# Reading the 512 moving columns of a matmul in 64-byte pieces, and shifting the operand tiles by 256 bytes against one pool of weights

## The chip, the cores and the metric

The kernel runs on one core of one Trainium2 chip. The metric is the device time of one execution in microseconds, the median of several runs. A core has a matrix engine (PE, whose weight loads the profile lists apart as PEld), a vector engine (DVE), a scalar engine (ACT), a general engine (POOL) and a sync engine (SP) that issues transfers. SBUF is the on-chip memory of 128 partitions from which the engines read operands, and PSUM is the accumulator memory into which PE writes.

## The reference, cut to what matters

One decoder layer on 1024 positions of width 1024, in float32:

```
h = rmsnorm(x)
[q | k | v | u | s | gate_a | gate_b] = h @ w_in
A = sliding-window attention(q, k, v);  B = u * (tril(W_s) @ rmsnorm(s) + b)
x = x + (sigmoid(gate_a) * (A @ w_oa) + sigmoid(gate_b) * (B @ w_ob)) @ w_out
x = x + down( silu(conv_g) * conv_v ),  conv = causal depthwise width-3 conv of up(rmsnorm(x))
```

The MLP is 2816 wide, so `w_up` has 5632 columns and `w_down` 2816 rows. All matrix products together are what PE does; every other operation is elementwise, a row reduction or a softmax over 128 keys.

## The kernel before, in words

**Arithmetic on PE.** Every float32 operand of a large product is split into a high part (`copy_hi`, line 77, on ACT) and a low part (a subtraction on POOL or DVE), both of type fp32r. A product is then three matmuls with one output: high weights by high moving, high weights by low moving, low weights by high moving. [...] The profile's group name `pz<-T,qh` reads: output `pz`, moving tile `T`, weight tile `qh`.

**Three places issue the 512-column matmuls.** `mm3` (lines 79 to 83) issues the three for the `u` projection (`pu`), the two branch outputs (`po`) and the `w_out` product (`px`). `Blocks.prod` (lines 924 to 929) issues twelve, four depth steps of three, for one of the seven block products into which the gate projections and the up projection are cut; its outputs are `pz`. `mms` (lines 1620 to 1633) does the same for the down projection, outputs `pd` and `pdy`. `mm3` also issues matmuls of 256 columns (`pkv`, `pq`, `pvs`, `pm`), and line 505 those of the attention output (`pv`).

**Stages.** The order is: key, value and first query projections; attention mixed with the rest of the query and `u` projections; the second token mixer; the gates in eight pairs; the branch outputs and `w_out`; the up projection in 22 pairs, each with convolution and gating of the pair before on ACT, DVE and POOL; the down projection in seven steps of eleven depth tiles. The order of PE's instructions is written out by hand; what is prepared for it (loads on SP's queue, high parts on ACT, low parts on POOL and DVE) runs some tiles ahead.

**Where the operands lie.** SBUF is handed out in pools from the left in the order `base` (line 44), `big` (line 47), `wst` (line 48), then the pools of the stages (`ex` and `wx` among them); `edge`, `gp` and `zr` come from the right. Each pool follows the end of the one before. `base` ends in a filler tile, `base_pad` (line 125), which makes it 7680 bytes, or 15 times 512, long; `edge_pad` does the like on the right. The tiles of `big`, `wst`, `ex`, `wx`, `gp` and `zr` that PE reads have sizes that are multiples of 512 bytes, so in the kernel before every weight tile and every moving tile of a 512-column matmul begins at a multiple of 512 bytes. `big` holds the moving tiles of nearly all products (`x`, `T`, `B`, `mh`, `ml`, `bh`, `bl`, `ah` and `al` as moving tiles of `po`), the weights of the down projection (`ah`, `al`), and `AX`, the weights of two of the seven block products. `wst` holds the weights `wuh`, `wul`, `wjh`, `wjl`, `ph`, `pl`, `qh`, `ql`. `gp` holds the gates' weights `gax` and `s3h`, `s3l`; `wx` holds the up projection's `s3h`, `s3l`, whose moving tile `T3` lies in `ex`. In the gates that moving tile lies in `zr`. The attention's tiles `ch`, `cl`, `eh`, `el`, moving in `pv`, begin 192 bytes past a multiple of 512, and their weights `vhl` at a multiple of 512.

Of the kernel before, what the change touches and what calls it, by code (L numbers as in the profile page):

```python
# [10 lines left out]
F = mybir.dt.float32  # L11
# [23 lines left out]
def build(tc, a):  # L35
    nc = tc.nc
    ctx = ExitStack()
    with ctx, tc.manual_schedule(engines={mybir.EngineType.PE}):
        body(ctx, tc, nc, a)


def body(ctx, tc, nc, a):
    L, H = slice(0, 512), slice(512, 1024)
    base = ctx.enter_context(tc.tile_pool(name="base", bufs=1))
# [3 lines left out]
    wst = ctx.enter_context(tc.tile_pool(name="wst", bufs=2))  # L48
    uid = [0]
    psum = {}  # L50

    def nm(s):
        uid[0] += 1
        return f"{s}_{uid[0]}"
# [18 lines left out]
    def raw(s):  # L73
        return wst.tile([128, 8, 128], F, tag="raw", name=nm(s), bufs=3)

    def copy_hi(dst, src, scale=1.0):
        return nc.scalar.activation(dst, src, AF.Copy, scale=scale)  # L77

    def mm3(out, wh, wl, mh, ml, first, last, **kw):

        nc.tensor.matmul(out, wh, mh, start=first, stop=False, **kw)  # L81
        nc.tensor.matmul(out, wh, ml, start=False, stop=False, **kw)  # L82
        nc.tensor.matmul(out, wl, mh, start=False, stop=last, **kw)  # L83
# [9 lines left out]
    def wsplit(r, s, nk=8):  # L93

        h = wst.tile([128, 8, 128], R, tag="wh", name=nm(s + "h"))
        l = wst.tile([128, 8, 128], R, tag="wl", name=nm(s + "l"))
        copy_hi(h[:, :nk, :], r[:, :nk, :])
        nc.gpsimd.tensor_tensor(l[:, :nk, :], r[:, :nk, :], h[:, :nk, :].bitcast(F), op=ALU.subtract)  # L98
        return h, l
# [22 lines left out]
    nsink = base.tile([128, 8], F, name="nsink")  # L122
    ss_b = base.tile([128, 8], F, name="ss_b")
    vss8 = base.tile([128, 8], F, name="vss8")
    base.tile([128, 72], F, name="base_pad")

    def rms_rows(pb, diag, hs=(0, 1)):

# [43 lines left out]
    def rsplit(w, r, c):  # L172

        rv = r.rearrange("p (k a) b -> p k (a b)", a=2)
        ks = slice(4 * c, 4 * c + 4)
        copy_hi(w[:, 0, ks, :], rv)
        nc.gpsimd.tensor_tensor(w[:, 1, ks, :], rv, w[:, 0, ks, :].bitcast(F), op=ALU.subtract)
# [33 lines left out]
    for k in range(8):  # L211
        x1 = xr[k]
        copy_hi(wkv[:, 0, k, :], x1[:, 1:257])
        nc.vector.tensor_tensor(wkv[:, 1, k, :], x1[:, 1:257], wkv[:, 0, k, :].bitcast(F), op=ALU.subtract)
        for c in xcuts[k] if k in xcuts else (slice(0, 512), slice(512, 1024)):
            xc = x1[:, 257 + c.start:257 + c.stop]
            copy_hi(hx(0, k, c), xc, scale=x1[:, 0:1])
            nc.vector.scalar_tensor_tensor(hx(1, k, c), xc, x1[:, 0:1], hx(0, k, c).bitcast(F),
                                           op0=ALU.mult, op1=ALU.subtract)
        for s in range(8):  # L220
            o = pkv[s // 4][:, (s % 4) * 256:(s % 4 + 1) * 256]
            c = slice(s * 128, (s + 1) * 128)
            mm3(o, hx(0, k, c), hx(1, k, c), wkv[:, 0, k, :], wkv[:, 1, k, :],
                k == 0 and s % 2 == 0, k == 7 and s % 2 == 1)
        if k > 0:
            xsquare(k - 1)
        if k + X_AHEAD < 8:
            xload(k + X_AHEAD)
        if k == 2:
            rwq = rload(a["wq"][0], "wq")  # L230
            nc.sync.dma_start(ident, a["ident"])
            nc.sync.dma_start(cp, a["cp"])
        if k == 4:
            u_raw = [wload(a["wu"][0], "wu")]
            nc.sync.dma_start(sink_b, a["sink"])
            nc.sync.dma_start(ali, a["ali"])
        if k == 5:
            rsplit(wq[0], rwq[0], 0)
        if k == 6:
            rsplit(wq[0], rwq[1], 1)  # L240
# [7 lines left out]
    def q_proj(n):  # L248
        half, b = divmod(n, 8)
        w = wq[half]  # L250
        p = PH("pq")[:, 0:256]
        c = slice(b * 128, (b + 1) * 128)
        for k in range(8):
            mm3(p, hx(0, k, c), hx(1, k, c), w[:, 0, k, :], w[:, 1, k, :], k == 0, k == 7)
        st[("pq", n)] = p
# [49 lines left out]
    for s in range(8):  # L305
        nc.tensor.matmul(p_ssq[:, 2 * s:2 * s + 2], sqsum[:, s * 128:(s + 1) * 128], ones[:, 0:2],
                         start=True, stop=True)
# [216 lines left out]
    def u_chunk(i):  # L524
        t, j = divmod(i, 4)
        if j == 0:
            ust["p"] = PS("pu")
        p, (wh, wl) = ust["p"], ust[("w", t)]
        for k in (2 * j, 2 * j + 1):
            for h in range(2):  # L530
                c = slice(h * 512, (h + 1) * 512)
                mm3(p[:, c], wh[:, k, :], wl[:, k, :], hx(0, k, c), hx(1, k, c), k == 0, k == 7)
        return t if j == 3 else None
# [382 lines left out]
    class Blocks:  # L916
# [7 lines left out]
        def prod(self, o, l, r, more=False):  # L924
            (wh, wl), y = self.w[l], self.y[r]
            for k in range(4):
                for j, (p, q) in enumerate(((wh, 0), (wh, 1), (wl, 0))):
                    nc.tensor.matmul(o, p[:, k, :], y[:, q, k, :], start=not more and k == 0 and j == 0,  # L928
                                     stop=k == 3 and j == 2, skip_group_check=True)

        def temps(self):
# [598 lines left out]
    def mlp():  # L1530
# [81 lines left out]
        def banks():  # L1612
            psum["C"].__exit__(None, None, None)
            ps = ctx.enter_context(tc.tile_pool(name="psD", bufs=1, space=bass.MemoryType.PSUM, reuse_waits="tile"))
            X.extend(ps.tile([128, 512], F, tag=f"pd{i}", name=f"pd{i}") for i in range(4))
            for _ in range(2):
                p = psA.tile([128, 1024], F, tag="P", name=nm("pdy"))
                Yb.extend([p[:, L], p[:, H]])

        def mms(g):  # L1620
            s, k0, k1 = groups[g]
            ah, al, bh, bl = ops_.pop(g)
            if g == 0:
                banks()
            o = Yb if s in ("M2", "M7", "M4") else X
            new = s in ("M1", "M7")
            for k in range(k0, k1):
                for d in range(4):
                    m = slice(128 * d, 128 * d + 128)
                    for j, (p, q) in enumerate(((ah, bh), (ah, bl), (al, bh))):  # L1630
                        nc.tensor.matmul(o[d], p[:, k - k0, m], q[:, k - k0, :],  # L1631
                                         start=new and k == 0 and j == 0, stop=k == HK - 1 and j == 2,
                                         skip_group_check=True)

# [61 lines left out]
        prev, q, rms = first_pair()  # L1696
        for n in range(1, NPAIR):
            q = fast_pair(n, prev, q or Pair(n, lefts[n].w), (start0, start1, start), rms)
            prev, q, rms = q, None, None
        q = prev  # L1700
        n_load = 4
        for g in range(len(groups)):
            mms(g)
            s, k0, k1 = groups[g]
            while n_load < min(g + 6, len(groups)):
                loads(n_load)
                n_load += 1
            if g in SUM_AT:
                sum_loads(*GR[SUM_AT.index(g)])
            if k1 == HK:  # L1710
                done(s)
            if g == 0:
                q.tap_v()
                q.last_sum()
                q.conv_v()
                prep(2)
                q.tap_g()
                q.conv_g()
            if g == 1:
                q.gated()  # L1720
                q.stores()
                pools["ft_cm"].__exit__(None, None, None)
                pools["yd"] = ctx.enter_context(tc.tile_pool(name="yd", bufs=1, reuse_waits="tile"))
            if g + 3 < len(groups):
                prep(g + 3)
            if g - 2 in SUM_AT:
                sums2(*GR[SUM_AT.index(g - 2)])
            if g == 0:
                q.tanh()
# [73 lines left out]
```

## Time and profile before

| | |
|---|---|
| time, median of 3 runs | 1197.96 us (1197.24 to 1198.21) |
| the profiled execution | 1196.57 us |
| its span in the trace | 1194.4 us |
| PE busy | 1181.5 us, 5850 matmuls |
| PEld busy | 999.1 us, 5850 weight loads |
| DVE, ACT, POOL busy | 864.3, 550.3, 561.3 us |
| HBM traffic | 159 GB/s over the span |

The span is the time from the first to the last instruction in the trace; the execution's own time is 2.17 us longer. Busy time of an engine is the union of its instructions' times, so matmuls that overlap in the pipeline are not counted twice. The duration of one matmul is from its start to its modelled end, and the next one starts long before that: what a matmul costs is the distance between two starts.

### The profile page before, as it was taken

How to read it: one execution, taken by the hardware profiler on the slowest of the kernel's cores; microseconds unless marked ns; L12 is line 12 of the kernel's file. 1: busy time of each engine (PE TensorE's matmuls, PEld its weight loads, DVE VectorE, ACT ScalarE, POOL GpSimd, SP SyncE). 2: the span in 40 equal slices, each digit the busy share in tenths (PEclk: the TensorE clock that was granted, in tenths of full speed). 3: DMA queues.
4: the chain of work that ended last, by engine and by line, in shares of the span. 5: the costliest groups of instructions: out<-in, count | busy, mean ns of one | idle time of the engine just before them, and what ended most of it. 6: DMA issues, size and time to landing. Idle time of an engine off the chain costs nothing.

```text
span 1194.4 us, 15778 instructions
## 1 busy us (share of the span) xinstructions
PE 1181.5 (99%) x5850; PEld 999.1 (84%) x5850; DVE 864.3 (72%) x1010; ACT 550.3 (46%) x848; POOL 561.3 (47%) x359
## 2 busy tenths in 40 slices
PE   9999999999999999999999999999999999999998
PEld 8889989888888888888888888888888888888887
DVE  8688967754548665347897788878887798865674
ACT  8455565744345222445544444444444445434331
POOL 2467683577768322334756575756656551000000
PEclk9999999999999999999999999999999999999999
DMA  7010133137786997343142333423233358965471
GB/s 286 21 54 19 54 129 128 36 99 245 247 313 215 352 317 269 146 150 115 54 141 99 113 128 110 141 91 131 106 133 112 100 203 285 384 229 194 145 234 71
DMA packets 78988, 191.00 MB, mean 160 GB/s; under 512 B 8896, under 2 KB 9152, under 8 KB 78912
## 3 DMA queue, kind: packets, MB, share of 16 engines
q1 hardware_dynamic: 78912, 190.00, 45.9%
q8 instruction: 46, 0.75, 0.3%
q14 instruction: 30, 0.25, 0.1%
HBM read 139.38 MB, written 50.59 MB: 159 GB/s over the span
## 4 chain that ended last, share of the span: by engine, by line
PE 91%; DVE 3%; ACT 1%; issue 0%; POOL 0%; ACTq 0%; DVEq 0%
PE pz L928 48%; PE pd L1631 10%; PE pdy L1631 8%; PE px L83 2%; PE px L81 2%; PE po L81 2%; PE po L83 2%; PE po L82 2%; PE px L82 2%; PE pvs L81 1%; PE pvs L83 1%; PE pvs L82 1%; PE pv L505 1%; PE pq L81 1%; PE pq L83 1%; PE pq L82 1%
## 5 line engine op out<-in xcount | busy, mean ns | idle before, releaser
L928 PE MATMUL pz<-T,qh 128*128 128x512 f32 x480 | 148.1, 390 | 0.0
L887 POOL TENSOR_TENSOR pl<-lp,ph 128x1024 fp32r<-128x1024 f32 x30 | 72.5, 2417 | 92.9 <-ACT ph L77 92.8
L928 PE MATMUL pz<-B,ph 128*128 128x512 f32 x352 | 109.7, 393 | 0.0
L928 PEld LDWEIGHTS pz<-T,qh 128*128 128x128 f32 x480 | 89.9, 188 | 18.5
L928 PE MATMUL pz<-T,ql 128*128 128x512 f32 x240 | 93.4, 389 | 0.0
L98 POOL TENSOR_TENSOR wjl<-wj,wjh 128x512 fp32r<-128x512 f32 (+1 forms) x24 | 40.7, 1697 | 102.1 <-ACT wjh L77 99.2
L887 POOL TENSOR_TENSOR ql<-lq,qh 128x1024 fp32r<-128x1024 f32 x29 | 74.9, 2583 | 8.8 <-ACT qh L77 8.8
L928 PEld LDWEIGHTS pz<-B,ph 128*128 128x128 f32 x352 | 65.3, 188 | 15.9 <-ACT x L1479 2.4
L943 DVE TENSOR_TENSOR pz<-pz,rstd_b 128x1024 f32<-128x1024 f32 x60 | 73.9, 1232 | 2.1
L887 POOL TENSOR_TENSOR s3l<-s,s3h 128x512 fp32r<-128x512 f32 x30 | 41.2, 1373 | 71.5 <-ACT s3h L77 71.5
L928 PE MATMUL pz<-T,s3h 128*128 128x512 f32 x240 | 73.9, 389 | 0.0
L928 PE MATMUL pz<-B,pl 128*128 128x512 f32 x176 | 68.5, 389 | 0.0
L1631 PE MATMUL pd<-bh,ah 128*128 128x512 f32 x176 | 68.5, 389 | 0.0
L1631 PE MATMUL pd<-bl,ah 128*128 128x512 f32 x176 | 68.5, 389 | 0.0
L1631 PE MATMUL pd<-bh,al 128*128 128x512 f32 x176 | 68.5, 389 | 0.0
L928 PE MATMUL pz<-B,AX 128*128 128x512 f32 x264 | 63.4, 389 | 0.0
L928 PE MATMUL pz<-T,AX 128*128 128x512 f32 x264 | 63.4, 389 | 0.0
L928 PEld LDWEIGHTS pz<-B,AX 128*128 128x128 f32 x264 | 49.6, 188 | 10.3
L928 PEld LDWEIGHTS pz<-T,AX 128*128 128x128 f32 x264 | 49.6, 188 | 10.3
L1337 DVE SCALAR_TENSOR_TENSOR tg<-pz,cp,tg 128x1023 f32<-128x1023 f32 (+1 forms) x44 | 56.2, 1278 | 0.8
L1337 DVE SCALAR_TENSOR_TENSOR tv<-pz,cp,tv 128x1023 f32<-128x1023 f32 (+1 forms) x44 | 56.2, 1278 | 0.8
L77 ACT ACTIVATE qh<-lq 128x1024 fp32r<-128x1024 f32 (+1 forms) x31 | 32.0, 1036 | 52.2 <-issue 24.7
(329 smaller groups left out, 3502.5 us busy)
## 6 DMA issues: line engine op xcount, KB each, us to landing
ls<-wup SPq DMA_DIRECT2D x22, 512.0 KB, 5.5
sum<-ls SPq DMA_DIRECT2D x22, 512.0 KB, 5.1
lp<-wup SPq DMA_DIRECT2D x22, 512.0 KB, 3.5
ra<-wdown SPq DMA_DIRECT2D x44, 256.0 KB, 4.5
b<-T SPq DMA_DIRECT2D x44, 256.0 KB, 3.7
B<-tv SPq DMA_DIRECT2D x33, 256.0 KB, 2.0
T<-tt SPq DMA_DIRECT2D x33, 256.0 KB, 2.0
b<-B SPq DMA_DIRECT2D x33, 256.0 KB, 3.7
```

Source lines behind the costliest of these rows:

```text
L77: return nc.scalar.activation(dst, src, AF.Copy, scale=scale)
L81: nc.tensor.matmul(out, wh, mh, start=first, stop=False, **kw)
L82: nc.tensor.matmul(out, wh, ml, start=False, stop=False, **kw)
L83: nc.tensor.matmul(out, wl, mh, start=False, stop=last, **kw)
L98: nc.gpsimd.tensor_tensor(l[:, :nk, :], r[:, :nk, :], h[:, :nk, :].bitcast(F), op=ALU.subtract)
L505: nc.tensor.matmul(o, vhl[:, kb, g, :], w, start=i == 0, stop=i == len(ops) - 1)
L887: nc.gpsimd.tensor_tensor(l, r, h.bitcast(F), op=ALU.subtract)
L928: nc.tensor.matmul(o, p[:, k, :], y[:, q, k, :], start=not more and k == 0 and j == 0, stop=k == 3 and j == 2, skip_group_check=True)
L943: nc.vector.tensor_tensor(z, z, rstd_b, op=ALU.mult)
L1337: nc.vector.scalar_tensor_tensor(t[:, j:], p[:, 0:1024 - j], cw[:, ci, 2 - j:3 - j], t[:, j:], op0=ALU.mult, op1=ALU.add)
L1631: nc.tensor.matmul(o[d], p[:, k - k0, m], q[:, k - k0, :], start=new and k == 0 and j == 0, stop=k == HK - 1 and j == 2, skip_group_check= ...
```

## The change

A helper `lines` views 512 columns as 4 blocks of 128 columns, each of 8 pieces of 16 columns, and walks them with the piece index outside and the block index inside. So PE takes 16 columns (64 bytes) at offset 0, then 64 bytes at offset 512, 1024 and 1536, then goes back to offset 64, and so on. The same view is put on the moving tile and on the PSUM output, so each column's sum lands where it did before, and whoever reads PSUM reads it as before. All three places that issue 512-column matmuls use it; in `mm3` a condition on the output's shape leaves the 256-column matmuls alone.

`base_pad` loses 64 elements (256 bytes), so every tile of `big` begins 256 bytes lower, half of 512 off; a tile `wst_pad` of 256 bytes is put first in `wst`, so the tiles of `wst` and of everything after it keep their addresses. No instruction is added or taken away on any engine, and no transfer changes in size.

```
+    wst.tile([128, 64], F, name="wst_pad", bufs=1)
...
+    def lines(t):
+        return t.rearrange("p (a b c) -> p b a c", a=4, b=8)
...
     def mm3(out, wh, wl, mh, ml, first, last, **kw):
+        if out.shape[1:] == (512,) or list(out.shape[1:]) == [512]:
+            out, mh, ml = lines(out), lines(mh), lines(ml)
...
-    base.tile([128, 72], F, name="base_pad")
+    base.tile([128, 8], F, name="base_pad")
...
-                    nc.tensor.matmul(o, p[:, k, :], y[:, q, k, :], start=not more and k == 0 and j == 0,
+                    nc.tensor.matmul(lines(o), p[:, k, :], lines(y[:, q, k, :]), start=not more and k == 0 and j == 0,
...
-                        nc.tensor.matmul(o[d], p[:, k - k0, m], q[:, k - k0, :],
+                        nc.tensor.matmul(lines(o[d]), p[:, k - k0, m], lines(q[:, k - k0, :]),
```

## The prediction

> **What bounds the kernel now.** I read the page first: the span, the busy shares, the granted clock and the chain of work that ended last.
>
> ```profile
> span 1194.4 us, 15778 instructions
> ...
> PE 1181.5 (99%) x5850; PEld 999.1 (84%) x5850; DVE 864.3 (72%) x1010; ACT 550.3 (46%) x848; POOL 561.3 (47%) x359
> ...
> PEclk9999999999999999999999999999999999999999
> ...
> PE 91%; DVE 3%; ACT 1%; issue 0%; POOL 0%; ACTq 0%; DVEq 0%
> ```
>
> PE is busy 99% of the span at the full granted clock and makes up 91% of the chain, so the time is the sum of PE's matmuls and little else. The table of busy time over the whole span, asked once for line 928, once for line 1631 and once each for the outputs px, po and pu, shows how much of that is touched (its columns: stretch, length, PE busy with the count, PEld busy with the count, then other engines, granted clock, DMA share, GB/s):
>
> ```profile
> 0.00:1194.40 1194.40, 574.75 (x2520) 471.76 (x2520) 1.00 0.46 160
> ...
> 0.00:1194.40 1194.40, 209.73 (x924) 173.30 (x924) 1.00 0.46 160
> ...
> 0.00:1194.40 1194.40, 87.20 (x384) 72.07 (x384) 18.44 (x17) 7.17 (x8) 1.00 0.46 160
> ...
> 0.00:1194.40 1194.40, 87.20 (x384) 72.07 (x384) 29.32 (x24) 1.00 0.46 160
> ...
> 0.00:1194.40 1194.40, 47.45 (x192) 34.87 (x192) 4.86 (x4) 1.00 0.46 160
> ```
>
> That is 2520 + 924 + 384 + 384 + 192 = 4404 matmuls of 512 columns and 1006.3 us of PE's 1181.5: one nanosecond on each is 4.4 us. A change of their order can only act through what one of them costs, so I went to the timeline of PE, and of the weight loads, at a place where PE goes from a steady run into a wait (columns: start in us, length in us, engine, line, operation):
>
> ```profile
> 736.67 0.62 PE L928 MATMUL pz<-T,s3h 128*128 128x512 f32 x2
> ...
> 737.80 0.39 PE L928 MATMUL pz<-T,s3l 128*128 128x512 f32 x1
> 738.03 0.71 PE L928 MATMUL pz<-B,ph 128*128 128x512 f32 x2
> 738.58 0.39 PE L928 MATMUL pz<-B,pl 128*128 128x512 f32 x1
> 738.81 0.62 PE L928 MATMUL pz<-B,ph 128*128 128x512 f32 x2
> ```
>
> ```profile
> 737.58 0.19 PEld L928 LDWEIGHTS pz<-T,s3l 128*128 128x128 f32 x1
> 738.01 0.30 PEld L928 LDWEIGHTS pz<-B,ph 128*128 128x128 f32 x2 [0.24 <-ACT x L1479]
> 738.35 0.19 PEld L928 LDWEIGHTS pz<-B,pl 128*128 128x128 f32 x1
> ```
>
> From 736.67 to 738.03 there are six starts (two, one, two, one), so a matmul costs 1.36 / 6 = 0.2267 us. I take 226.7 ns as the steady price; 4404 of them are 998.4 us. Now the matmul at 737.80. Weight loads normally run beside a matmul, one ahead. Here the load that ended at 737.58 + 0.19 = 737.77 was the last until 738.01: the next waited 0.24 us for ACT. The matmul at 737.80 therefore streamed almost alone, and the next one still starts 0.23 us later. Its duration says the same. The list of line 928 for that instant, for the steady stretch 730 to 736 us and for the stretch just after the wait (durations least/median/most, ns):
>
> ```profile
> L928 PE MATMUL pz<-T,s3l x1: 388/388/388, 737.8 to 737.8; 128*128 128x512 f32 x1
> ```
>
> ```profile
> L928 PE MATMUL pz<-B,AX x12: 389/389/389, 729.9 to 732.4; 128*128 128x512 f32 x12
> ```
>
> ```profile
> L928 PE MATMUL pz<-B,ph x3: 389/395/479, 738.0 to 738.8; 128*128 128x512 f32 x3
> L928 PE MATMUL pz<-B,pl x1: 393/393/393, 738.6 to 738.6; 128*128 128x512 f32 x1
> ```
>
> Alone 388 ns, in the steady run 389, just after a wait 393 to 395 (the 479 includes the wait for its own weights). So a weight load beside a matmul costs about 1 ns when the two have settled, and 4 to 6 ns while they have not. What lies under the 226.7 ns without any load beside it stays.
>
> **The floor.** How much could one matmul lose at the very best? The row nearest to that is the plain float32 matmul of line 130 (timeline row, then its durations):
>
> ```profile
> 580.84 1.88 PE L130 MATMUL pz<-diag,ones 128*128 128x512 f32 x4
> ```
>
> ```profile
> L130 PE MATMUL pz<-diag,ones x4: 592/592/592, 580.8 to 582.1; 128*128 128x512 f32 x4
> ```
>
> Four of them take 1.88 us to the end of the last, so three distances are 1.88 - 0.592 = 1.288, or 429.3 ns each; half of that is 214.7 ns. No row shows 512 columns cheaper than this half, so 226.7 - 214.7 = 12.0 ns is the most I allow as a gain: 52.8 us over 4404.
>
> **The change part by part.** It adds no instruction, so every term is a price per matmul times a count. Its own baseline is the profiled execution: 1194.4 us of span and 2.17 us around it, 1196.57, which is 1.39 us below the median of the runs.
>
> Step 1, the 256 bytes. All tiles of `big` move by half of 512 against everything else, so a pair of moving tile and weight tile changes its relation only if one of the two lies in `big` and the other doesn't. Pairs that keep it are both in `big` (line 1631, and the weights `AX`) or both outside (the weights `s3h` and `s3l`). The groups by form give the counts:
>
> ```profile
> L928 PE MATMUL pz<-T,s3h 128*128 128x512 f32 x240 | 73.9, 389 | 0.0
> ...
> L928 PE MATMUL pz<-B,AX 128*128 128x512 f32 x264 | 63.4, 389 | 0.0
> L928 PE MATMUL pz<-T,AX 128*128 128x512 f32 x264 | 63.4, 389 | 0.0
> ...
> L928 PE MATMUL pz<-T,s3l 128*128 128x512 f32 x120 | 46.8, 390 | 0.0
> ```
>
> 924 + 528 + 360 = 1812 matmuls keep a relation of 0 and 2592 get 256. For the 2592 the settled cost of the load beside them, 389 - 388 = 1 ns, can go: at most 2.6 us, and I take half, -1.3 us. The ends are -12.0 ns (the floor) and +6 ns (395 - 389, unsettled), -31.1 to +15.6 us.
>
> That a byte offset between the two operands matters at all, one place in the trace shows. In the timeline of the attention the moving tiles of `pv` lie 192 bytes off their weights, those of `pq` 0:
>
> ```profile
> 90.97 0.28 PE L505 MATMUL pv<-ch,vhl 128*128 128x256 f32 x1
> ...
> 91.42 0.28 PE L81 MATMUL pq<-wq,x 128*128 128x256 f32 x1
> ...
> 92.00 0.28 PE L83 MATMUL pq<-wq,x 128*128 128x256 f32 x1
> ...
> 92.48 0.28 PE L81 MATMUL pq<-wq,x 128*128 128x256 f32 x1
> ```
>
> Four `pv` take 0.45 us, 112.5 ns each; four `pq` take 0.48, 120 ns. Two weight loads with nothing before them start 0.30 - 0.19 = 0.11 us apart (the row at 738.01), as long as a matmul of 256 columns; so I read the 7.5 ns as a load that is held up, and with 512 columns there is room for it. [...]
>
> Step 2, the 192 matmuls of 256 columns whose moving tile `wvB` lies in `zr` and whose weights `x` lie in `big`. They are not permuted, but get the offset of 256:
>
> ```profile
> L81 PE MATMUL pvs<-wvB,x 128*128 128x256 f32 x64 | 18.2, 284 | 0.0
> L82 PE MATMUL pvs<-wvB,x 128*128 128x256 f32 x64 | 18.1, 283 | 0.0
> L83 PE MATMUL pvs<-wvB,x 128*128 128x256 f32 x64 | 18.1, 283 | 0.0
> ```
>
> Between -7.5 ns (like `pv`) and the same upwards: 192 x 7.5 = 1.4 us either way. I take -3 ns, -0.6 us, since the one other offset in the trace helped.
>
> Step 3, the order itself on all 4404. The read keeps whole runs of 64 bytes and the PSUM write gets the same runs; no row shows a 512-column matmul with such an order. Nearest below is the floor, -12.0 ns. Nearest above: each of the 32 runs costs one more column's time, 226.7 / 512 = 0.443 ns, so 14.2 ns, 62.4 us; far above, a write at the pace of the 429.3 ns matmul, 202.6 ns, 892 us. I take 0, since the lone matmul shows a price that is not from the load, and nothing in the trace ties it to the order of addresses.
>
> Step 4, the 1812 pairs at relation 0, whose moving tile now stays four times as long at each offset within 512. Settled they cost 0 to 1 ns today; ends -12.0 and +6 ns, -21.7 to +10.9 us; I take 0.
>
> Other engines do not come up as a bound. In the stretch of the gates, outputs and up projection they have a quarter free, more than the 6% that PE could win:
>
> ```profile
> 230.00:980.00 750.00, 749.55 (x3325) 618.79 (x3325) 536.17 (x518) 320.57 (x388) 430.80 (x227) 1.00 0.47 164
> ```
>
> (DVE is 536.17 of 750.) Waits before PE are tenths of a microsecond and stay. The sum is 1196.57 - 1.3 - 0.6 = 1194.7 by the profiled execution and 1196.1 by the median; I say **1196**: no change that can be told.
>
> **The rivals.** *The price hangs on the step from one 64-byte piece to the next* (faster). Today a matmul changes its offset within 512 bytes 32 times, permuted 8 times. If the 12.0 ns are paid per change, three quarters go: 9.0 x 4404 = 39.6 us, 1158; all of it would give 1145, and if only the 2592 pairs set apart win it all, 1167. For it speaks that 256 columns settle at 112.5 ns, half of 226.7 within 1 ns, so the price grows with the columns, as one per piece would; against it that nothing shows adjacency as the cause.
>
> *Pairs at relation 0 meet* (slower). The weights of 1812 matmuls and their moving tile begin at the same offset, and the moving tile no longer runs away from it. If they never settle, each pays 4 to 6 ns as after a wait: 7.2 to 10.9 us, **1207**; if the 2592 don't settle either, 4404 x 6 = 26.4, 1224. It decides wherever the settled 226.7 is lost. For it: 393 to 395 with unchanged tiles, only the moment shifted. [...]
>
> *The runs cost something by themselves* (slower): 1260 by 14.2 ns. [...] No row of this trace shows it.
>
> *The change does not reach its aim*: where weights and moving tile both lie in `big` the offset does nothing, in 41% of the matmuls; that is in steps 1 and 4.
>
> **How the numbers follow.** No change by the sum: 0.36, of which 0.10 are a gain of more than 0.2% (the ends of step 1). Price per piece: 0.29. Pairs meet: 0.20. Runs cost: 0.15. A difference of 0.2%, 2.4 us, is about what a measurement of this kernel can tell from none. So faster 0.29 + 0.10 = 0.39, same 0.26, slower 0.20 + 0.15 = 0.35. The likeliest case alone reaches from 1192 to 1200. Since cases of both signs hold most of the chance, the range goes down to 1152, past the 1158 of three quarters, and up to 1232, past 1224; outside are the case of the runs and the gain of the whole 12 ns, about 0.2.
>
> **What would show it.** Step 3 right: six starts of line 928 still 1.36 us apart, durations 388 to 389. Price per piece: starts near 217 ns and durations near 380 in all groups alike. Step 1 alone: the groups with weights `ph`, `qh`, `wjh` shorter than those with `AX` and `ah`. Pairs meet: `AX`, `s3h` and line 1631 at 393 or more and the others at 389. Runs cost: all groups longer by the same amount, PE's busy share unchanged. Step 2: `pvs` with `wvB` some 3 to 7 ns below 283. The prediction is wrong if any large group moves by over 2 ns.

## The result: slower by 1.6%, in every permuted matmul alike

The changed kernel takes 1216.66 us (median; 1214.29 to 1218.92) beside 1197.60 us for the kernel before (1197.1 to 1198.21), four runs each: a ratio of 1.0159, 95% interval 1.0133 to 1.0184, or 19.1 us. The page of the profile after, with the lines that answer to those read before:

```profile
span 1212.1 us, 15785 instructions
...
PE 1199.7 (99%) x5850; PEld 1001.4 (83%) x5850; DVE 862.3 (71%) x1010; ACT 552.7 (46%) x848; POOL 556.9 (46%) x359
...
PEclk9999999999999999999999999999999999999999
...
PE 90%; DVE 4%; ACT 1%; issue 1%; POOL 0%; DVEq 0%; ACTq 0%
```

PE is as full as before and at the full granted clock; its busy time grew by 1199.7 - 1181.5 = 18.2 us, the span by 17.7, and no other engine's busy time by more than 2.4. Where the 18.2 lie shows in the busy time over the whole span, asked for lines 935 and 1638 (928 and 1631 before) and for the outputs px, po and pu (columns as in the prediction):

```profile
0.00:1212.10 1212.10, 584.68 (x2520) 473.21 (x2520) 1.00 0.46 158
...
0.00:1212.10 1212.10, 213.77 (x924) 173.56 (x924) 1.00 0.46 158
...
0.00:1212.10 1212.10, 88.91 (x384) 72.19 (x384) 18.44 (x17) 7.17 (x8) 1.00 0.46 158
...
0.00:1212.10 1212.10, 88.91 (x384) 72.19 (x384) 29.33 (x24) 1.00 0.46 158
...
0.00:1212.10 1212.10, 48.06 (x192) 34.93 (x192) 4.85 (x4) 1.00 0.46 158
```

The five sum to 1024.3 us, against 1006.3: 18.0 of the 18.2 us are in the 4404 permuted matmuls, 4.1 ns on each in this execution. Each row grew, by 1.3% (pu) to 2.0% (px and po), whatever its operands. The groups by form say how:

```profile
L935 PE MATMUL pz<-T,s3h 128*128 128x512 f32 x240 | 74.7, 392 | 0.0
L1638 PE MATMUL pd<-bh,ah 128*128 128x512 f32 x176 | 69.7, 396 | 0.0
L1638 PE MATMUL pd<-bh,al 128*128 128x512 f32 x176 | 69.7, 396 | 0.0
...
L1638 PE MATMUL pd<-bl,ah 128*128 128x512 f32 x176 | 68.2, 388 | 0.0
L935 PE MATMUL pz<-T,AX 128*128 128x512 f32 x264 | 64.6, 393 | 0.0
...
L88 PE MATMUL px<-mh,wjh 128*128 128x512 f32 x128 | 49.6, 387 | 0.0
```

Before, these stood at 389 and 390. Now two of three matmuls show 396 ns and one 387 or 388. Groups of line 935 show the mean of that (392, 393), since there weights such as `qh` serve at two places of the three. The timeline of PE in the down projection (start, length, engine, line, operation):

```profile
1000.00 0.40 PE L1638 MATMUL pd<-bh,ah 128*128 128x512 f32 x1
1000.24 0.39 PE L1638 MATMUL pd<-bl,ah 128*128 128x512 f32 x1
1000.47 0.40 PE L1638 MATMUL pd<-bh,al 128*128 128x512 f32 x1
1000.70 0.40 PE L1638 MATMUL pd<-bh,ah 128*128 128x512 f32 x1
...
1001.85 0.40 PE L1638 MATMUL pd<-bh,al 128*128 128x512 f32 x1
```

From 1000.00 to 1001.85 there are eight distances: 231 ns each instead of 226.7. They repeat in threes, 235, 227 and 232 ns by the exact starts. In px the short one is `mh` on `wjh`, the first of its three products, in pd `bl` on `ah`, the second: the cycle of three belongs to the stream of matmuls and not to one pair of tiles. This is the profile of an execution of 1214.29 us; the median is higher, because the executions lie in two clusters, of which more at `e2_order`.

### The profile page after: what moved, and what is told of

Read it like the earlier page. It is cut to its first block, busy times and chain, and to the rows that moved or that the text cites. A ratio compares the mean times of both kernels' runs of the same rounds, so it can differ in the third digit from the quotient of the medians.

```text
span 1212.1 us, 15785 instructions
## 1 busy us (share of the span) xinstructions
PE 1199.7 (99%) x5850; PEld 1001.4 (83%) x5850; DVE 862.3 (71%) x1010; ACT 552.7 (46%) x848; POOL 556.9 (46%) x359
## 4 chain that ended last, share of the span: by engine, by line
PE 90%; DVE 4%; ACT 1%; issue 1%; POOL 0%; DVEq 0%; ACTq 0%
PE pz L935 48%; PE pd L1638 10%; PE pdy L1638 8%; PE px L89 2%; PE po L89 2%; PE po L90 2%; PE px L90 2%; PE po L88 2%; PE px L88 2%; PE pvs L88 1%; PE pvs L90 1%; PE pvs L89 1%; PE pq L88 1%; PE pq L90 1%; PE pq L89 1%; PE pv L512 1%
## 5 line engine op out<-in xcount | busy, mean ns | idle before, releaser
L950 DVE TENSOR_TENSOR pz<-pz,rstd_b 128x1024 f32<-128x1024 f32 x60 | 73.9, 1232 | 2.4 <-ACT rstd_b L139 0.4
```

The lines of the kernel that those rows point to most:

```text
L950: nc.vector.tensor_tensor(z, z, rstd_b, op=ALU.mult)
```

## The experiments

### One part of the change at a time

`e1_offset` keeps the shift of 256 bytes and reads in plain order:

```
     def lines(t):
-        return t.rearrange("p (a b c) -> p b a c", a=4, b=8)
+        return t
```

> The places of the change (big 256 bytes lower, wst_pad) with the old order of columns. Theory ORDER (the permuted order by itself costs 4.3 ns on each of the 4404 matmuls of 512 columns, whatever the weights' place): as before, 1197 us, starts 226.7 ns apart in every group. Theory PLACE (what counts is where moving tile and weights lie against each other): the groups with weights in wst go to 231 ns, those with AX and line 1631 stay at 226.7, about 1208 us.

Measured: 1197.60 us beside 1198.29, ratio 0.9996 (0.9987 to 1.0005). The groups by form are those of the kernel before:

```profile
L1638 PE MATMUL pd<-bh,ah 128*128 128x512 f32 x176 | 68.5, 389 | 0.0
...
L935 PE MATMUL pz<-T,AX 128*128 128x512 f32 x264 | 63.4, 389 | 0.0
```

The shift neither costs nor brings anything, in the pairs that it moves apart as in the others.

`e2_order` keeps the order and takes the shift back:

```
-    wst.tile([128, 64], F, name="wst_pad", bufs=1)
...
-    base.tile([128, 8], F, name="base_pad")
+    base.tile([128, 72], F, name="base_pad")
```

> The permuted order on the moving tiles and on PSUM, with every tile at its old address. Theory ORDER: as after, 1217 us, starts 231.2 ns apart on the mean, in a cycle of about 235, 227 and 232 ns, in every group. Theory PLACE: the 2592 pairs that the change set apart now meet too, so slower than after, above 1220 us; or, if the offset was what hurt, back to 1197 us.

Measured: 1219.83 us (1214.62 to 1220.59), ratio 1.0168 (1.0141 to 1.0194). The order alone is the whole loss. In the profiled execution the groups are long as after the change, at other sizes in part:

```profile
L1637 PE MATMUL pd<-bh,ah 128*128 128x512 f32 x176 | 69.4, 394 | 0.0
...
L934 PE MATMUL pz<-T,AX 128*128 128x512 f32 x264 | 65.1, 393 | 0.0
...
L89 PE MATMUL px<-mh,wjl 128*128 128x512 f32 x128 | 49.6, 387 | 0.0
```

Its executions, like those of the changed kernel, lie in two clusters, near 1214.5 and from 1218.5 to 1220.6 us. The profiled one is of the upper cluster (span 1218.2), and by the starts of its matmuls it runs at two paces. Up to 588.9 us it shows the cycle of three of the changed kernel (231.1 ns on the mean; `px` lies in this part). There four plain float32 matmuls and a wait interrupt the stream. From 590.8 to 1122.4 us the matmuls take an even 233.3 ns, with durations of 393; after a longer distance of 278 ns the cycle of three returns. The even stretch has some 2280 matmuls, each 2.2 ns dearer, which makes 5.0 us, about the distance of the two clusters. The changed kernel's profile has the cycle of three alone. What decides which pace follows an interruption, the runs do not show.

`e3_read_only` takes the shift back too, permutes the moving tile alone and leaves PSUM in plain order.

```
-            out, mh, ml = lines(out), lines(mh), lines(ml)
+            mh, ml = lines(mh), lines(ml)
...
-                    nc.tensor.matmul(lines(o), p[:, k, :], lines(y[:, q, k, :]), ...
+                    nc.tensor.matmul(o, p[:, k, :], lines(y[:, q, k, :]), ...
```

> The permuted order on the moving tile alone, old addresses; PSUM is written in plain order, so the columns of a product come out permuted and the output is not the reference's. If the cost is on the read side: starts 231 ns apart, about 1217 us. If it is on PSUM's write side: starts 226.7 ns apart, 1197 us.

Measured, timed once: 1214.9 us beside 1198.29. Its groups are the changed kernel's:

```profile
L1637 PE MATMUL pd<-bh,ah 128*128 128x512 f32 x176 | 69.8, 396 | 0.0
L934 PE MATMUL pz<-T,s3h 128*128 128x512 f32 x240 | 74.8, 392 | 0.0
```

So the loss is paid where the moving tile is read; that the permuted PSUM columns have no part in it rests here on one execution, and the next run tests it by itself.

### Is 256 bytes a special distance?

That e1 changed nothing could mean that places don't matter, or that 256 bytes is a whole period of what matters. `m1_matmuls` is no layer but rows of 36 matmuls on PE alone, one row for each order, place and size, with weights and moving tiles at chosen addresses:

```
        run("read", four)                     # moving tile permuted, PSUM plain
        run("write", same, four)              # PSUM permuted, moving tile plain
        for e, n in ((16, "e"), (32, "f"), (48, "g"), (64, "h"), ...):
            run("woff" + n, woff=e)           # weights e elements (4 bytes) further
        for na, nb, n in ((4, 4, "d"), (4, 2, "e"), (2, 16, "f"), ...):
            v = pieces(na, nb)
            run("cut" + n, v, v)
```

> Not the layer: rows of 36 matmuls after one another on PE alone, one row per form (the output tile is named after the form: seq plain; both, read, write the permuted order on both sides or one; woff weights 64 to 448 bytes off; moff moving tile 64 bytes off; bothoff permuted and weights 256 bytes off; cut other lengths of piece; wnarrow and wthin weights of 64 and 32 columns; c fewer columns; b bfloat16; rowshalf 64 partitions). Nothing else runs then, so other engines' reads are out. Theory ORDER: seq 226.7 ns from start to start, both and bothoff 231, woff all 226.7. Theory PLACE: woff differ by several ns. [...]

The busy time of one row at a time, in this order: plain; moving tile and PSUM permuted as in the change; moving tile alone; PSUM alone; weights 64, 128, 192 and 256 bytes further; then pieces of 256 bytes, pieces of 64 bytes taken in turn from two blocks of 1024 bytes (16 columns out of each 256), and the change's order in bfloat16:

```profile
0.00:303.90 303.90, 8.32 (x36) 6.76 (x36) 0.98 0.07 28
0.00:303.90 303.90, 8.50 (x36) 6.77 (x36) 0.98 0.07 28
0.00:303.90 303.90, 8.48 (x36) 6.77 (x36) 0.98 0.07 28
0.00:303.90 303.90, 8.35 (x36) 6.76 (x36) 0.98 0.07 28
0.00:303.90 303.90, 8.56 (x36) 6.77 (x36) 0.98 0.07 28
0.00:303.90 303.90, 8.53 (x36) 6.78 (x36) 0.98 0.07 28
0.00:303.90 303.90, 8.41 (x36) 6.76 (x36) 0.98 0.07 28
0.00:303.90 303.90, 8.34 (x36) 6.76 (x36) 0.98 0.07 28
0.00:303.90 303.90, 8.36 (x36) 6.76 (x36) 0.98 0.07 28
0.00:303.90 303.90, 8.80 (x36) 6.84 (x36) 0.98 0.07 28
0.00:303.90 303.90, 7.93 (x36) 0.98 0.07 28
```

Busy time is 35 distances and one duration (389 to 403 ns by the row's group). The plain row gives (8.32 - 0.389) / 35 = 226.6 ns; the change's order gives 231.6, the moving tile alone 231.1, PSUM alone 227.4 (226.7 once the first few are past). Weights 64, 128, 192 and 256 bytes further: 233.3, 232.4, 229.1 and 227.2. At 320, 384 and 448 bytes the three prices come again, so the pattern repeats every 256 bytes. Pieces of 256 bytes are free (227.7, and 226.7 once the first few are past); 64-byte pieces from two blocks cost more than the change's from four (239.9); bfloat16 has 215.7 ns, plain or permuted. Weights of 32 columns, whose load takes 109 ns instead of 188, do not lower the price of a plain row but raise it (8.51 us, 231.7 ns). Rows of 256 and 384 columns take 120.0 and 173.3 ns beside 226.7 for 512: 53.3 for each 128, and some 13 over at each of the three lengths. In these rows PE works alone (from 37 to 150 us, where most of them lie, ACT and POOL are busy for 0.00 us and the DMA share is 0.00), and the change's order costs what it costs in the layer (231.1 to 231.6 ns here, 231 there): no other engine's access and no transfer is needed for it.

`e4_offset128` puts that to the layer: plain order, but 128 bytes instead of 256.

```
-    wst.tile([128, 64], F, name="wst_pad", bufs=1)
+    wst.tile([128, 32], F, name="wst_pad", bufs=1)
...
-        return t.rearrange("p (a b c) -> p b a c", a=4, b=8)
+        return t
...
-    base.tile([128, 8], F, name="base_pad")
+    base.tile([128, 40], F, name="base_pad")
```

> Plain order, the tiles of big and those of wst 128 bytes apart within 512 in place of 256 (base_pad 40, wst_pad 32 elements). Theory PERIOD 256 (weight load and moving tile disturb each other by their places within 256 bytes, so that 256 is the same as 0 and 128 is as far off as can be): the 2592 pairs at 232.4 ns in place of 226.7, the other 1812 unchanged, 14.8 us more, about 1212 us. Rival NO PLACE (the layer's matmuls don't feel the place at all): 1197 us.

Measured: 1213.77 us beside 1197.87, ratio 1.0128 (1.0113 to 1.0143). The groups by form part in the main as the pairs do:

```profile
L935 PE MATMUL pz<-T,qh 128*128 128x512 f32 x480 | 151.0, 395 | 0.0
...
L1638 PE MATMUL pd<-bh,ah 128*128 128x512 f32 x176 | 68.5, 389 | 0.0
...
L935 PE MATMUL pz<-T,AX 128*128 128x512 f32 x264 | 64.2, 392 | 0.0
L935 PE MATMUL pz<-B,AX 128*128 128x512 f32 x264 | 63.6, 390 | 0.0
...
L88 PE MATMUL px<-mh,wjh 128*128 128x512 f32 x128 | 50.6, 395 | 0.0
```

Weights of `wst` against moving tiles of `big`, now 128 bytes apart, rise from 389 to 395; pd, both operands in `big`, stays. `AX` lies in `big` too, yet its groups rise a little, and the starts say why. The twelve matmuls of `B` by `AX` take 226.7 ns each as before, all but the last: at the 20 places where a product with `ph` comes next, that last one takes 232.5 ns (duration 396), with its own two tiles still at a difference of 0. What changed for it is the load that runs beside it, that of `ph`. So what counts is where the moving tile lies against the weights that are being loaded for the next matmul. `T` by `AX`, which follows a product with `qh`, starts disturbed and needs some eight matmuls to settle. The 15.9 us over the 2592 shifted pairs are 6.1 ns each, this carry-over included, beside 5.7 for 128 bytes in the row above. So the shift by 128 bytes cost 1.3% of this layer, and the change's 256 bytes cost nothing (ratio 0.9996 in e1).

`e5_order128` is the changed kernel with those 128 bytes (the two pads of e4, the order as in the change).

> The permuted order with 128 bytes between big and wst in place of 256. Theory PERIOD 256: the 2592 pairs at about 236 ns, the 1812 at 231.1, so 1197.6 + 2592 x 9.3 + 1812 x 4.4 = 1230 us. Rival STREAM ALONE (the order's cost is in the moving read and no place changes it): as after, 1217 us. If the offset of 128 is what the order needs: under 1205 us.

Measured: 1228.42 us, ratio 1.0252 (1.0236 to 1.0267), from its groups:

```profile
L935 PE MATMUL pz<-T,qh 128*128 128x512 f32 x480 | 152.3, 398 | 0.0
...
L1638 PE MATMUL pd<-bh,ah 128*128 128x512 f32 x176 | 68.9, 392 | 0.0
```

Order and place add up, in part: 30.5 us beside 19.1 and 15.9 for each alone. By the starts `px`, at 128 bytes, takes 236.0 ns, and the down projection, at 0, on the whole the 231 of the order alone.

`e6_wide` keeps the change's shift and its idea, but moves in pieces of 64 columns, 256 bytes:

```
-        return t.rearrange("p (a b c) -> p b a c", a=4, b=8)
+        return t.rearrange("p (a b c) -> p b a c", a=4, b=2)
```

> The same edit with pieces of 64 columns (256 bytes of every 512) in place of 16. Theory PERIOD 256 (within a piece the read walks through all four 64-byte places in turn, as the plain order does): no cost, 1197 us, starts 226.7 ns apart. Rival ANY JUMP (each break in the order of addresses costs, 8 pieces in place of 32): a quarter of after's loss, about 1202 us.

Measured: 1197.46 us, ratio 0.9996 (0.9986 to 1.0006), and every large group is back:

```profile
L1638 PE MATMUL pd<-bh,ah 128*128 128x512 f32 x176 | 68.5, 389 | 0.0
```

A permuted order costs nothing as such: from the same four blocks, pieces of 256 bytes are free (0.9996) and pieces of 64 are not (1.0159). The size alone does not decide either, for 64-byte pieces cost 4.4 ns from four blocks and 13.3 from two (m1).

### The price by place, and the price alone

`m2_places` lays a grid over both addresses, in steps of 64 bytes: eight places of the moving tile by four of the weights, 28 matmuls each, then the two orders at four places.

```
        for m_ in range(8):
            for w_ in range(4):
                if m_ or w_:
                    run("g" + L[m_] + L[w_], moff=16 * m_, woff=16 * w_)
```

> Not the layer: rows of 28 matmuls after one another, as in the first such run. Groups g: moving tile and weights each 0 to 448 and 0 to 192 bytes off (first letter a to h: the moving tile in steps of 64 bytes; second letter a to d: the weights in steps of 64). four, step, stepq: 16 columns of every 128, 256 and 64, each with weights 0 to 192 bytes off. h: 256 columns. n: fewer columns. lone: one matmul at a time, its weights written by ACT from the result of the one before, so that no weight load runs beside it. Theory PAIR (moving tile and weight load collide where they stand at the same 64 bytes within 256): cost depends on the difference of the two places alone, the order four is cheap at some difference, and lonefour lasts as long as loneseq. Theory STREAM (the order costs in the moving read itself): four costs 231 ns at every difference, and lonefour lasts some 10 ns longer than loneseq. If any group falls under 224 ns, it is worth trying in the layer.

Groups by form (first letter after the g: place of the moving tile, second: of the weights, from a in steps of 64 bytes; aa is the plain row; four is the change's order, step the 64-byte pieces from two blocks):

```profile
L54 PE MATMUL pstepa<-mv,wt 128*128 128x512 f32 x28 | 6.9, 403 | 0.0
...
L54 PE MATMUL pfourb<-mv,wt 128*128 128x512 f32 x28 | 6.8, 399 | 0.0
...
L54 PE MATMUL pgab<-mv,wt 128*128 128x512 f32 x28 | 6.7, 395 | 0.0
...
L54 PE MATMUL pgba<-mv,wt 128*128 128x512 f32 x28 | 6.6, 391 | 0.0
...
L54 PE MATMUL pgbb<-mv,wt 128*128 128x512 f32 x28 | 6.5, 390 | 0.0
```

The price goes by the difference of the two places, in 256 bytes: from start to start, once a row has settled, 226.7 ns at 0 (aa, bb, cc, dd, and the same 256 bytes on), 233.3 with the weights 64 bytes ahead, 232.4 at 128. At 64 behind the difference alone does not tell it: 228.8 (ba, cb) or 233.3 (dc, ad), and m1 had 229.1 at the places of ad. Steps of 64 bytes are not the grain: a moving tile 16 bytes off takes 231.7, weights 16 bytes off 226.7. The change's order with the weights 0, 64, 128 and 192 bytes ahead has 231.1, 236.7, 236.0 and 236.6, that is 4.4 ns above the plain row at 0 and some 3.5 at the others; step has 240.0 at all four, so there the place adds nothing. No place and no order had 512 fp32r columns under 226.6 ns, so there was no version to run that would beat both kernels. The groups with idle gaps between the matmuls ran while the granted clock was not full (0.94 over the span), the plain form at 707 ns on the mean and the other 512-column forms at 779, and tell nothing here.

Is the order's price one of the read itself, or of the weight load that runs beside it? `m3_lone` leaves out the load beside one matmul in nine.

> Not the layer: groups of nine matmuls, the weights of the first written by ACT from the seventh of the group before, so that the ninth of each group streams with no weight load beside it while PE stays warm. seq plain; four, step, wide, big the permuted order in pieces of 16 columns of every 128, 16 of every 256, 32 of every 128, 64 of every 128; read the order on the moving side alone; off the moving tile 128 bytes off; thin weights of 32 columns. Theory PAIR (the order costs because it meets the weight load): the ninth lasts 388 ns in every form, and with thin weights the order costs next to nothing. Theory STREAM (the order costs in the moving read itself): the ninth lasts 388 ns in seq and big and off, and 395 or more in four and step, with thin weights too.

The matmul without a load beside it took 388 ns in plain order, 392 or 397 alternating in the change's and in the read-only one, 403 in step; but the plain order 128 bytes off also showed 397 and 388 in turn, with nothing beside it to meet. So a duration here still carries a lag from its neighbour, and m3 does not decide by it. Its rows with weights of 32 columns speak for the load: 231.7 ns plain and 232.0 in the change's order, so with a shorter load the order adds 0.3 ns instead of 4.4, though both stand above the plain row's 226.7. `m4_alone` therefore puts each matmul behind its own new weights, with PE idle before it and no load beside it (duration, own load included):

```
                fresh(p)                      # ACT writes new weights: PE must wait
                nc.tensor.matmul(vo(p[:, 0, 0:cols]), wl[turn[0]], vm(mv[:, moff:moff + cols]), ...)
                fresh(p)
```

> Not the layer: runs of 16 plain matmuls that keep PE warm, and between two of them a single matmul whose own weights, and those of the next, are written by ACT after the matmul before. So before the single one PE is idle, and beside it no weight load runs; nothing can be carried into it from a neighbour. The output tile names its form: seq plain; four the change's order, read and write the order on one side; step 16 of every 256 columns; wide 32 of every 128; big 64 of every 128; off and offs plain with the moving tile 128 and 64 bytes off; two and three with 256 and 384 columns. Theory PAIR: all 512-column forms last the same, and the order costs only where a load runs beside it. Theory STREAM: four, step and wide last 4 to 14 ns longer than seq here too, off and offs do not. For the 13 ns above 512 columns: if two, three and seq differ by 53.3 ns for each 128 columns, they are a fixed price of each matmul; if by 56.7, a price of each column.

```profile
L74 PE MATMUL pstep<-mv,wl 128*128 128x512 f32 x8 | 4.1, 507 | 3.4 <-ACT wl L63 3.4
L74 PE MATMUL poffs<-mv,wl 128*128 128x512 f32 x8 | 4.0, 505 | 3.4 <-ACT wl L63 3.4
...
L74 PE MATMUL pread<-mv,wl 128*128 128x512 f32 x8 | 4.0, 501 | 3.4 <-ACT wl L63 3.4
...
L74 PE MATMUL pseq<-mv,wl 128*128 128x512 f32 x8 | 4.0, 494 | 3.4 <-ACT wl L63 3.4
...
L74 PE MATMUL pwrite<-mv,wl 128*128 128x512 f32 x8 | 4.0, 494 | 3.4 <-ACT wl L63 3.4
L74 PE MATMUL pthree<-mv,wl 128*128 128x384 f32 x8 | 3.5, 438 | 3.4 <-ACT wl L63 3.4
L74 PE MATMUL ptwo<-mv,wl 128*128 128x256 f32 x8 | 3.1, 382 | 3.4 <-ACT wl L63 3.4
```

With no next load beside it the permuted read costs 501 - 494 = 7 ns and the permuted PSUM write 0. So the order has a price in the read without the next weights' load; the record of the matmul's own load, 186 ns long, still overlaps its first part, and m4 can't take that out. In the steady row 4.4 of these 7 are seen, with thin weights 0.3; how the two combine there, the runs do not show. A plain read 64 bytes off costs 11 ns alone (505), 128 bytes off 1 ns (495, which the plain form's second group also shows). In a row the same places cost 2.1 and 5.7 (228.8 at ba and 232.4 at 128 bytes in m2, beside 226.7), and nothing when the weights are shifted along (226.7 at bb). So a place has two effects: one is the load beside, from e4 and m2; the other, the 11 ns, I can't name.

## Why the prediction was wrong, by its own steps

**Step 3, the order, failed.** It was taken as 0 "since the lone matmul shows a price that is not from the load, and nothing in the trace ties it to the order of addresses". The observation held, the conclusion didn't: that no row tied the price to the order was no evidence that it isn't tied, for no row had another order. Measured: +4.4 ns in a steady row, +7 alone, 18.0 us in the layer's 4404 by the profile, 19.1 by the clock. It lay inside the bounds that I gave (-12.0 to +14.2), and the mechanism is the rival *the runs cost something by themselves*, which I gave 0.15: all groups longer alike, PE's share unchanged. That the time lies between 1152 and 1232 is luck: the upper end was set for a case that did not happen, and the one that did was left outside, at 1260. Two things in that rival were off. Its size, one column's time for each of the 32 pieces, was three times too much: 4.4 / 32 is 0.14 ns for a piece. And the write into PSUM, for which step 3 allowed up to 892 us, has no part in it (e3, m1, m4).

**Step 1, the shift, gave 0 instead of -1.3 us** (e1), and not for the reason that made it small. I took a settled load to cost about 1 ns wherever it lies, and counted by a matmul's own weights. By place it costs 0 to 6.7 ns, the weights of the next matmul count, and the kernel before stood at the one of the four places, in steps of 64 bytes, where it costs nothing; 256 bytes is the next such place. The upper end that I gave, +6 ns for each of the 2592 pairs, 15.6 us, happens to be what 128 bytes would have brought (15.9 in e4); it was argued from the moments after a wait, not from places.

**Step 2 gave 0 instead of -0.6 us.** The 192 matmuls with `wvB` stand at 283 and 284 ns as before. The row that I argued from, `pv` at 192 bytes and 112.5 ns, said something of 192 bytes; I carried it to 256, which is again a difference of 0. The row was a fast one besides: over the whole trace of the kernel before, two neighbouring `pv` start 116 ns apart in the median, and m2 has 117.8 for 256 columns 192 bytes off. At 128 bytes (e4) the `wvB` matmuls did get 1 ns shorter.

**Step 4 gave no term of its own.** The pairs at relation 0 (`AX`, `s3h`, pd) got longer by the same as the others, so the rival *pairs at relation 0 meet* falls, although 1207 and 1224 lie on both sides of the time; in e6 the same pairs stand at 389 in another permuted order. The rival *price per piece* (faster) falls with the sign: the matmul that changes its place four times less often got longer. What lies above my floor of 214.7 ns stays open. In a row, 256, 384 and 512 columns take 120.0, 173.3 and 226.7 ns (m1): 53.3 for each 128 and some 13 over at each of the three lengths, so 256 columns are not half of 512 as that rival had it. Alone, 128 columns more cost 438 - 382 = 56 and 494 - 438 = 56 ns (m4), which would make 224 of the 226.7 a price of the columns. The two do not agree.

**What held.** The weight of one nanosecond (4.4 us) and the claim that a change of order acts only through what one matmul costs: no other engine, queue or wait took part. So did the list of what would show each step; all groups long alike was there under its rival's name.

**The weight load and PSUM.** Of the weight load, the traces show 389 ns beside a load and 388 without in plain order, but 395 with the operands 128 bytes apart (e4). So at the places of the kernel before a load beside a matmul shows as 1 ns, e1's groups have the same 389, and in e4 a change of place alone costs 1.3%, paid beside the load. Of PSUM, the row written in 64-byte pieces took 227 ns (m1) and, alone, the same 494 as the plain one (m4), while the read in 64-byte pieces costs 7 ns alone (m4).

## What to carry to other kernels

An experiment on one matmul form belongs before a forecast of "no change": where a kernel is 99% PE, 4 ns that no row shows are 1.6%, and an order or a place that the trace never had is unknown, not free. For fp32r matmuls of 512 columns like these, keep moving tiles in plain order or in runs of 256 bytes (1197.46 us in e6, 1216.66 with runs of 64), and put a moving tile at the same place modulo 256 bytes as the weights that load beside it, those of the next matmul (226.7 ns, and 228.8 to 233.3 at the other steps of 64 bytes, m2); the order of PSUM columns is free in runs of 64 bytes (494 ns either way, m4). When a shift does nothing, try half of it before saying that places don't matter.

## What the runs showed of the hardware that I had not expected

- The price of a steady stream of 512-column matmuls like this kernel's goes by the difference of its two SBUF addresses modulo 256 bytes: 226.7, 233.3, 232.4, and 228.8 or 233.3 ns at 0, 64, 128 and 192 (m2). The address that counts is that of the weights loading beside the matmul (e4). A stream of 256 columns does it the other way round: 120 ns at 0 and 117.8 to 118.7 elsewhere (m2).
- A moving tile read in 64-byte pieces from four blocks costs 4.4 ns in a row (m2) and 7 alone (m4); from two blocks 13.3 and 13. From four blocks, pieces of 256 bytes cost nothing in a row, pieces of 128 bytes 6.6 and of 32 bytes 4.5 (m1), so more pieces are not always dearer.
- The extra time comes at two paces, a cycle of three matmuls (235, 227 and 232 ns) and an even 233.3; one stream can change from one to the other at an interruption (e2), and executions of one program fall into two clusters about as far apart as that makes (1214.5 and 1219 us).
- Less weight does not help: 32 columns of weights, loaded in 109 ns, take 231.7 ns instead of 226.7 (m1). bfloat16 has 215.7 ns in either order (m1).
- Left open: why a read 64 bytes off costs 11 ns with nothing beside it (505 and 494, m4), and what stands behind the 256 bytes. The runs show the period, not its cause.
